# A two-layer hybrid block on one core: fewer, packed loads at the start, and the first two projections interleaved

## The chip, the core and the metric

The kernel runs on one core of a Trainium2 chip. TensorE (PE) multiplies, VectorE (DVE), ScalarE (ACT) and GpSimd (POOL) work element by element, and SyncE (SP) issues nearly all loads. The metric is the device time of one execution in microseconds.

## The reference

Two layers. Each normalises the stream (256 context and 256 latent tokens of 1024 channels), scales and shifts it by a modulation vector, projects it by one wide matrix, runs three token mixers on the parts (a state-space scan, "SSD", differential attention, and an mLSTM), and merges them by gates:

```
shift, scale, gate = split(silu(c) @ w_mod + b_mod, 3)       # c_ctx for the context tokens
h = rms_norm(x, norm_g) * (1 + scale) + shift
p = split_cols(h @ w_in, IN_SIZES)     # x, B, C, z, dt, q, k, v, ..., ig, fg, gates
ya = ssd_branch(p[0], p[1], p[2], ...)      # conv + silu of x, B, C; dt; a scan in both directions
yb = diff_branch(...);  yc = mlstm_branch(...)
mixed = sum_i sigmoid(gates_i) * (y_i @ w_branch[i])
x = x + gate * (mixed @ w_out)
```

## The kernel before

Every product in float32 is made of three products of float32r halves: a weight tile `raw` is rounded to `whi` by ACT (L117), DVE subtracts to get `wlo` (L83, the helper `tt`), and the stream h likewise has `hh` and `hl`. A **granule** is half a weight block: 4 of the 8 slices of 128 input channels by 256 columns, 512 KB, loaded into one of three `raw` buffers. `proj_ch` (L164) makes two blocks of 128 output channels by 512 tokens from two granules, 24 matmuls of 512 columns for each granule (lines L177 to L179).

The start of layer 0 is `mod_pair` (L243): twice eight loads of `w_mod` (512 KB, `wm`), each followed at once by its two matmuls (`mod_mm`, L226), which lay slice k into column tile k mod 4 of one PSUM bank. ACT copies the bank (`modrow`, L262), and `mod_tail` (L235) folds the four column tiles into modulation columns `modc`. The first pair gives shift and scale for slices 0 to 3 of h, the second for slices 4 to 7. The last three loads of the second pair go into `raw` buffers. Between the `wm` loads `few_loads` issues the small parameters: rows of `prow` (bias, conv weights and gains, later turned into columns by `columns`, L395), and the tables of `narrow` (L287: `gcol`, `gctx`, `dbc`, `lamt`) and `rope`.

`turn` (L488) transposes normalised tokens (L493), applies modulation on ACT (`hf`), rounds on POOL (`hh`) and subtracts on DVE (`hl`). Then come the gate matmuls (L553 to L555) on the narrow weights `wsm`, six loads of 4 or 16 columns (L544); a long chain on their 64 rows (L586 to L649) gives the SSD's decays, and its first use of PE is the transpose at L627. The blocks follow in the order `bc_proj(0)`, `x_proj(0, 0)`, `x_proj(0, 1)`, `ssd_core(0)`, the q, k, v blocks, and the same for the second group.

The order on every engine is made by a scheduler before the run, from priorities: the bands put loads and evacuations first (0), mixer work second (1) and the matmuls of projections last (2), so that these fill what the others leave free. On the chip each engine keeps that order. Every load in turn takes one of eight completion counters, and SP issues it only when the load eight places earlier has landed. PSUM has three banks `acc`, three `pe` and two `pm`.

Of the kernel before, what the change touches and what calls it, by code (L numbers as in the profile page):

```python
# [18 lines left out]
D = 1024  # L19
P = 128  # L20
# [9 lines left out]
NR = 64  # L30
ACC, PE_, PM = 3, 3, 2
# [3 lines left out]
def hybrid_backbone_kernel(ctx: ExitStack, tc: tile.TileContext, A, out, dbg=None):  # L35
# [128 lines left out]
    def proj_ch(srcs, lhs, ranges, evac, halves=False, gr=None):  # L164
# [3 lines left out]
        with band(2):  # L168
            for i in range(2):
                ps.append(pacc())  # L170
# [11 lines left out]
        if not halves:  # L182
            for k0, hi, lo in gr:
                with band(2):
                    for i in range(2):
                        go(i, k0, hi, lo, *ranges[i], True, True)
        else:
# [8 lines left out]
        for i in range(2):  # L196
            with band(0):
                evac(i, ps[i])

# [31 lines left out]
    def mod_tail(l, cbs, row):  # L231
        with band(2):
# [3 lines left out]
            for x, cb in enumerate(cbs):  # L236
                r = 16 * l + 12 + cb // 3
# [5 lines left out]
    def mod_pair(l, cbs, pool, bufs, rbufs, between=None, each=None, end=False):  # L243
        with band(2):
            ps = pacc()
            for x, cb in enumerate(cbs):
                if x and between:
                    between()
                for k0 in range(0, KT, 2):
                    if end and x and k0 >= 2:  # L250
                        wm = mk(wts, [P, 2, 512], "raw", bufs=3)
                    else:
                        wm = mk(pool, [P, 2, 512], "wm", bufs=bufs)
# [6 lines left out]
                    mod_mm(ps, x, k0, wm)  # L260
# [26 lines left out]
    def narrow(l, pool):  # L287
# [3 lines left out]
        lamt = mk(pool, [P, 4, 64], "lamt", bufs=1)  # L291
        lp = mk(pool, [P, 2, 64], "lp", bufs=1)
# [47 lines left out]
    prow = [mk(setup, [16, 1536], f"prow{l}") for l in range(depth)]  # L340
    with band(0):
# [5 lines left out]
        for l in range(depth):  # L347
            V.memset(prow[l], 0.0)
# [3 lines left out]
        few = []  # L352
        for l in range(depth):
            w_ = prow[l]

            few += [
                (w_[12:14, :], A["b_mod"][l].rearrange("(a n) -> a n", a=2)),
                (w_[8:9, 0:D], A["norm_g"][l : l + 1]),
                (w_[0:3, :], A["ssd_conv_w"][l]),
                (w_[3:4, :], A["ssd_conv_b"][l : l + 1]),  # L360
                (w_[4:7, 0:D], A["ml_conv_w"][l]),
                (w_[7:8, 0:D], A["ml_conv_b"][l : l + 1]),
                (w_[9:10, 0:D], A["ssd_norm_g"][l : l + 1]),
                (w_[10:11, 0:D], A["ml_norm_g"][l : l + 1]),
                (w_[11:12, 0:P], A["diff_subln_g"][l : l + 1]),
            ]
# [9 lines left out]

# [15 lines left out]
    def columns(l):  # L392
        pc = pm()
        for k in range(12):
            T.transpose(pc[:, 16 * k : 16 * k + 16], prow[l][:, k * P : (k + 1) * P], ident[0:16, 0:16])  # L395
        pl_ = pcols[:, :, 16 * l : 16 * l + 16]
        V.tensor_copy(pl_, pc[:, 0:192].rearrange("p (k a) -> p k a", a=16))

        tsc(pl_[:, :, 0:8], pl_[:, :, 0:8], 0.5, ALU.mult)
        lam_init = 0.8 - 0.6 * math.exp(-0.3 * l)  # L400
        tsc(pl_[:, 0, 11:12], pl_[:, 0, 11:12], 0.5 * (1.0 - lam_init), ALU.mult)
# [1013 lines left out]
```

## Time and profile before

| | us |
|---|---|
| median of three runs (lowest, highest) | 1688.14 (1687.44, 1690.84) |
| the profiled execution, and its span | 1688.44, 1686.7 |
| PE busy | 1649.9 |
| mean granted TensorE clock | 0.992 |

The times are to be read with the profile's own terms: a span runs from the first to the last instruction, a busy engine works on something, and an instruction's row names what ended the idle time ahead of it. Matmul records overlap, so a full PE still has its pace in the distance between starts: 0.227 us for a matmul of 512 columns at the full clock.

### The profile page before, as it was taken

Reading aid. Unit: us, or ns where it says so; the run is one execution under the profiler, and the core shown is the slowest. Engines: PE = TensorE matmul, PEld = TensorE weight load, DVE = VectorE, ACT = ScalarE, POOL = GpSimd, SP = SyncE. Lnnn points to the kernel's source line nnn. Section 1 sums busy time; section 2 is a strip of 40 time slices with the busy share of each in tenths; the row PEclk is TensorE's granted clock in tenths of the full one; section 3 lists DMA queues with packets and bytes.
Section 4 is the critical chain, followed back from the end, with each engine's and each line's share of the span. In section 5 each row is a group of like instructions: output and inputs, shape, how many; then the busy total and the mean of one; then the engine's idle time right before and its main releaser. Section 6 shows DMA issues by size and latency. Waiting matters only on the chain. (4 is left out here: it accounts for less than half of the span.)

```text
span 1686.7 us, 28784 instructions
## 1 busy us (share of the span) xinstructions
PE 1649.9 (98%) x11288; PEld 1470.5 (87%) x11288; DVE 1093.0 (65%) x2175; ACT 765.4 (45%) x1497; POOL 185.1 (11%) x232
## 2 busy tenths in 40 slices
PE   6999999999999999999999999999999999999998
PEld 2798789999899999977777789988899999999998
DVE  4787887767864776523334355796887767775565
ACT  3467534554554543422223233556455555444453
POOL 0114331001100000000010001022122011000100
PEclk8999999999999999999999999999999999999999
DMA  8445322222223222453544442344342325336654
GB/s 273 119 134 160 88 79 79 69 71 63 78 63 101 79 85 64 128 187 93 182 136 128 161 135 59 93 127 135 107 116 76 100 76 141 110 101 176 183 168 150
DMA packets 203653, 197.00 MB, mean 117 GB/s; under 512 B 21855, under 2 KB 184033, under 8 KB 203517
## 3 DMA queue, kind: packets, MB, share of 16 engines
q1 hardware_dynamic: 203516, 195.16, 39.4%
q8 instruction: 89, 1.46, 0.3%
q14 instruction: 48, 0.39, 0.1%
HBM read 193.29 MB, written 1.84 MB: 116 GB/s over the span
## 5 line engine op out<-in xcount | busy, mean ns | idle before, releaser
L83 DVE TENSOR_TENSOR wlo<-raw,whi 128x1024 fp32r<-128x1024 f32 x274 | 347.1, 1267 | 313.8 <-ACT whi L117 312.4
L147 PE MATMUL acc<-wlo,hh 128*128 128x256 f32 x1728 | 504.4, 292 | 0.0
L146 PE MATMUL acc<-whi,hh 128*128 128x256 f32 x1728 | 502.3, 291 | 0.0
L148 PE MATMUL acc<-whi,hl 128*128 128x256 f32 x1728 | 501.5, 290 | 0.0
L117 ACT CAST whi<-raw 128x1024 fp32r<-128x1024 f32 x274 | 287.1, 1048 | 378.1 <-PE acc L178 253.0
L147 PEld LDWEIGHTS acc<-wlo,hh 128*128 128x128 f32 x1728 | 330.1, 191 | 12.5 <-issue 9.5
L148 PEld LDWEIGHTS acc<-whi,hl 128*128 128x128 f32 x1728 | 330.2, 191 | 12.2 <-issue 10.6
L146 PEld LDWEIGHTS acc<-whi,hh 128*128 128x128 f32 x1728 | 329.8, 191 | 11.0 <-issue 8.5
L177 PE MATMUL acc<-hh,whi 128*128 128x512 f32 (+1 forms) x712 | 254.1, 359 | 1.3 <-DVE cv_a L80 1.3
L178 PE MATMUL acc<-hl,whi 128*128 128x512 f32 (+1 forms) x712 | 253.7, 357 | 0.2 <-DVE hl L83 0.2
L179 PE MATMUL acc<-hh,wlo 128*128 128x512 f32 (+1 forms) x712 | 253.1, 357 | 0.0
L177 PEld LDWEIGHTS acc<-hh,whi 128*128 128x128 f32 x712 | 135.0, 191 | 28.3 <-issue 5.9
L178 PEld LDWEIGHTS acc<-hl,whi 128*128 128x128 f32 x712 | 135.4, 190 | 19.4 <-issue 2.4
L179 PEld LDWEIGHTS acc<-hh,wlo 128*128 128x128 f32 x712 | 135.3, 190 | 19.3 <-issue 1.8
L177 PE MATMUL acc<-yh,whi 128*128 128x512 f32 (+1 forms) x384 | 128.7, 338 | 0.0
L178 PE MATMUL acc<-yl,whi 128*128 128x512 f32 (+1 forms) x384 | 128.2, 336 | 0.0
L179 PE MATMUL acc<-yh,wlo 128*128 128x512 f32 (+1 forms) x384 | 128.1, 336 | 0.0
L179 PEld LDWEIGHTS acc<-yh,wlo 128*128 128x128 f32 x384 | 71.9, 188 | 8.3
L178 PEld LDWEIGHTS acc<-yl,whi 128*128 128x128 f32 x384 | 72.1, 188 | 8.0
L968 ACT ACTIVATE E<-pe,nmax 128x512 f32<-128x512 f32 (+1 forms) x96 | 58.7, 616 | 44.8 <-DVE nmax L966 44.6
L177 PEld LDWEIGHTS acc<-yh,whi 128*128 128x128 f32 x384 | 72.0, 188 | 7.3
L811 ACT ACTIVATE ex<-ex,col 128x128 f32<-128x128 f32 x192 | 60.4, 393 | 34.8 <-POOL ex L766 31.0
(302 smaller groups left out, 2429.3 us busy)
## 6 DMA issues: line engine op xcount, KB each, us to landing
raw<-in_w_in_dram SPq DMA_DIRECT2D x192, 512.0 KB
raw<-in_w_branch_dram SPq DMA_DIRECT2D x48, 512.0 KB
wm<-in_w_mod_dram SPq DMA_DIRECT2D x45, 512.0 KB
raw<-in_w_in_dram SPq DMA_DIRECT2D x48, 256.0 KB
ex<-acs_d SPq DMA_DIRECT2D x32, 256.0 KB
raw<-in_w_out_dram SPq DMA_DIRECT2D x16, 512.0 KB
ex<-acs_d SPq DMA_DIRECT2D x32, 128.0 KB
pw<-nm_d SPq DMA_DIRECT2D x8, 256.0 KB
```

What stands on the lines that cost most here:

```text
L83: (eng or V).tensor_tensor(out=o, in0=a, in1=b, op=op)
L117: S.copy(hi, raw)
L146: T.matmul(o, lhsT=xh[:, k, sl], rhs=hi[:, j, :], start=(k == 0 and i == 0), stop=False)
L147: T.matmul(o, lhsT=xh[:, k, sl], rhs=lo[:, j, :], start=False, stop=False)
L148: T.matmul(o, lhsT=xl[:, k, sl], rhs=hi[:, j, :], start=False, stop=(k == KT - 1 and i == 1))
L177: T.matmul(o, lhsT=hi[:, j, cs], rhs=xh[:, k, a:b], start=(k == 0 and first), stop=False)
L178: T.matmul(o, lhsT=hi[:, j, cs], rhs=xl[:, k, a:b], start=False, stop=False)
L179: T.matmul(o, lhsT=lo[:, j, cs], rhs=xh[:, k, a:b], start=False, stop=(k == KT - 1 and final))
L811: S.activation(ex[:, c, :], ex[:, c, :], AF.Exp, bias=col[:, LDT, c, d, h : h + 1])
L968: S.activation(e_, o, AF.Exp, bias=ng[:, m : m + 1], accum_out=rs[:, m : m + 1])
```

## The change

The parameter rows of both layers are loaded together, ten loads in the place of eighteen, into `mrow_` (modulation bias and norm gain) and `prow` (the rest), with column numbers `C_CW` to `C_NORM` in the place of `16 * l + r`. The tables of `narrow(0)` and `rope` move from between the modulation loads to behind them. The gate weights come in two loads (32 and 16 columns) into `wnr`, and three DVE copies put them into `wsm`, in both layers. All modulation loads have buffers of their own (11 `wm`), and `mod_pair` holds one load back, so that two loads' matmuls, four column tiles, stand together. The first granule of `x_proj(0, 0)` is loaded ahead of the second modulation pair, like that of `bc_proj(0)`; the two blocks of layer 0 alternate by granules, the second one in `pe` banks. `turn` in layer 0 goes slice by slice over both halves of the tokens and uses `pm` banks alone.

```diff
+    mrow_ = mk(setup, [6, 1536], "mrow_")
+    prow = mk(setup, [22, 1536], "prow")
-    prow = [mk(setup, [16, 1536], f"prow{l}") for l in range(depth)]
...
-            few += [
-                (w_[12:14, :], A["b_mod"][l].rearrange("(a n) -> a n", a=2)),
-                (w_[8:9, 0:D], A["norm_g"][l : l + 1]),
-                (w_[0:3, :], A["ssd_conv_w"][l]),
...
-            if l == 0:
-                few += [(selm, A["k_selm"]), (sgn, A["k_sgn"])]
-                nar = narrow(0, setup)
-                few += nar[0]
-                few += [(rope, A["k_rope"].rearrange("a t p d -> p a t d"))]
+        few = [
+            (mrow_[0:4, :], A["b_mod"].rearrange("l (a n) -> (l a) n", a=2)),
+            (mrow_[4:6, 0:D], A["norm_g"]),
+            (selm, A["k_selm"]),
+            (prow[0:6, :], A["ssd_conv_w"].rearrange("l k n -> (l k) n")),
+            (prow[6:8, :], A["ssd_conv_b"]),
+            (prow[8:14, 0:D], A["ml_conv_w"].rearrange("l k n -> (l k) n")),
+            (prow[14:16, 0:D], A["ml_conv_b"]),
+            (prow[16:18, 0:D], A["ssd_norm_g"]),
+            (prow[18:20, 0:D], A["ml_norm_g"]),
+            (prow[20:22, 0:P], A["diff_subln_g"]),
+            (sgn, A["k_sgn"]),
+        ]
...
     def mod_pair(...):
+                held = []
                 for k0 in range(0, KT, 2):
-                    if end and x and k0 >= 2:
-                        wm = mk(wts, [P, 2, 512], "raw", bufs=3)
-                    else:
-                        wm = mk(pool, [P, 2, 512], "wm", bufs=bufs)
+                    wm = mk(pool, [P, 2, 512], "wm", bufs=bufs)
...
-                    mod_mm(ps, x, k0, wm)
+                    held.append((k0, wm))
+                    if len(held) == 2:
+
+                        for k_, w_ in held:
+                            mod_mm(ps, x, k_, w_)
+                        held = []
...
-    mods = [mod_pair(0, (0, 2), setup, 8, 2, load_x, lambda: few_loads(2))]
-
-    first_gr = granules(bc_cols(0, 0))
-    first_gr = chain([next(first_gr)], first_gr)
+    mods = [mod_pair(0, (0, 2), setup, 11, 2, load_x, lambda: few_loads(1))]
+
+    first_gr = [granules(bc_cols(0, 0)), granules([A["w_in"][0][:, O_X : O_X + 256]])]
+    first_gr = [chain([next(g)], g) for g in first_gr]
     mods += [
-        mod_pair(0, (1, 3), setup, 8, 2, None, lambda: few_loads(3), end=True),
+        mod_pair(0, (1, 3), setup, 11, 2, None, lambda: few_loads(1)),
     ]
     with band(0):
+        columns(mrow_, 22)
         few_loads(99)
-        columns(0)
+        columns(prow, 0)
...
             def turn(kh, s):
-                for k in range(4 * kh, 4 * kh + 4):
-                    pt = (pe if k % 2 else pm)()[:, 0:256]
+                for k in kh:
+                    pt = (pe if k % 2 and l else pm)()[:, 0:256]
...
-                    for s in range(2):
-                        turn(kh, s)
+                    for k in range(4 * kh, 4 * kh + 4):
+                        for s in range(2):
+                            turn((k,), s)
...
+            wnr = mk(wts, [P, KT, 48], "raw", bufs=3)
             wsm = mk(wts, [P, KT, P], "raw", bufs=3)
             V.memset(wsm, 0.0)
-            pieces = ((0, O_DT, 16), (16, O_FG, 4), (32, O_DT + 16, 16), (48, O_FG + 4, 4), (80, O_IG, 4), (112, O_IG + 4, 4))
-            for c, o, n in pieces:
-                nc.sync.dma_start(wsm[:, :, c : c + n], w_in[:, o : o + n].rearrange("(k p) n -> p k n", p=P))
+            for c, o, n in ((0, O_DT, 32), (32, O_IG, 16)):
+                nc.sync.dma_start(wnr[:, :, c : c + n], w_in[:, o : o + n].rearrange("(k p) n -> p k n", p=P))
+
+            v4 = lambda a: a.rearrange("p k (d r) -> p k d r", d=2)
+            for c, o, n in ((0, 0, 16), (16, 40, 4), (80, 32, 4)):
+                h_ = 64 * (c // 64)
+                V.tensor_copy(v4(wsm[:, :, h_ : h_ + 64])[:, :, :, c % 64 : c % 64 + n], v4(wnr[:, :, o : o + 2 * n]))
+            if l == 0:
+
+                scr = mk(wts, [P, 1024], "raw", bufs=3)
...
+                for p_ in nar[0][4:] + nar[0][:4]:
+                    nc.sync.dma_start(*p_)
+                nc.sync.dma_start(rope, A["k_rope"].rearrange("a t p d -> p a t d"))
...
+            first = l + g + b == 0
+            return proj_ch([wcol(O_X + 512 * g + 256 * b)], hT, [(0, 512)] * 2, f, gr=first_gr[1] if first else None, bank=pe if first else None)
...
-        bc_proj(0)
-        x_proj(0, 0)
-        x_proj(0, 1)
+        if l == 0:
+            run(zip_longest(bc_proj(0), x_proj(0, 0)))
+        else:
+            run(bc_proj(0))
+            run(x_proj(0, 0))
+        run(x_proj(0, 1))
```

What the scheduler makes of it shows in the order of three engines. SP in the second modulation pair, first before: `wm` and the last `raw` are modulation loads, all others small.

```order
L255 DMA wm<-in_w_mod_dram 128x2x512
L375 DMA prow_99<-in_norm_g_dram 1x1024
L375 DMA prow_99<-in_ssd_conv_w_dram 3x1536
L375 DMA prow_99<-in_ssd_conv_b_dram 1x1536
L255 DMA wm<-in_w_mod_dram 128x2x512
L375 DMA prow_99<-in_ml_conv_w_dram 3x1024
L375 DMA prow_99<-in_ml_conv_b_dram 1x1024
L375 DMA prow_99<-in_ssd_norm_g_dram 1x1024
L255 DMA raw<-in_w_mod_dram 128x2x512
L375 DMA prow_99<-in_ml_norm_g_dram 1x1024
L375 DMA prow_99<-in_diff_subln_g_dram 1x128
L255 DMA raw<-in_w_mod_dram 128x2x512 x2
```

The same place now; `raw` are the two first granules.

```order
L260 DMA wm<-in_w_mod_dram 128x2x512
L378 DMA prow<-in_ml_conv_w_dram 6x1024
L260 DMA wm<-in_w_mod_dram 128x2x512
L378 DMA prow<-in_ml_conv_b_dram 2x1024
L260 DMA wm<-in_w_mod_dram 128x2x512
L378 DMA prow<-in_ssd_norm_g_dram 2x1024
L130 DMA raw<-in_w_in_dram 128x4x128 x2
L130 DMA raw<-in_w_in_dram 128x4x256
L260 DMA wm<-in_w_mod_dram 128x2x512
L378 DMA prow<-in_ml_norm_g_dram 2x1024
L260 DMA wm<-in_w_mod_dram 128x2x512
L378 DMA prow<-in_diff_subln_g_dram 2x128
```

Two or three small loads stood between two modulation loads, and now one; the granule for x has come in.

PE in the first blocks, before: L177 to L179 are the B/C block, L553 to L555 the gates, L395 the row columns of layer 1.

```order
L553 MATMUL pe<-hh,whi 128x512
L554 MATMUL pe<-hl,whi 128x512
L555 MATMUL pe<-hh,wlo 128x512
L179 MATMUL acc<-hh,wlo 128x512
L177 MATMUL acc<-hh,whi 128x512
L178 MATMUL acc<-hl,whi 128x512
L395 MATMUL pm<-ident,prow_99 128x16 x12
L553 MATMUL pe<-hh,whi 128x512
L554 MATMUL pe<-hl,whi 128x512
L555 MATMUL pe<-hh,wlo 128x512
L553 MATMUL pe<-hh,whi 128x512
```

Now: L492 are transposes of x, L565 to L567 the gates, L179 to L181 the B/C block in `acc` and the x block in `pe`.

```order
L492 MATMUL pm<-ident,xin 128x128 x4
L565 MATMUL pe<-hh,whi 128x512
L179 MATMUL acc<-hh,whi 128x512 x2
L566 MATMUL pe<-hl,whi 128x512
L567 MATMUL pe<-hh,wlo 128x512
L180 MATMUL acc<-hl,whi 128x512
L181 MATMUL acc<-hh,wlo 128x512
L180 MATMUL acc<-hl,whi 128x512
L181 MATMUL acc<-hh,wlo 128x512
L179 MATMUL pe<-hh,whi 128x512
L180 MATMUL pe<-hl,whi 128x512
L179 MATMUL pe<-hh,whi 128x512
```

The gate matmuls, once in two runs of four slices, now go slice by slice between those of two blocks, and transposes of x have moved in.

DVE about the second set of modulation columns (`modc`, `ga`), before; `raw` here is the zeroed tile of gate weights.

```order
L83 TENSOR_TENSOR hl<-hf,hh 128x256 x8
L541 MEMSET raw 128x1024
L83 TENSOR_TENSOR modc<-acc,pcols 128x8 x2
L87 TENSOR_SCALAR ga<-modc 128x8
L83 TENSOR_TENSOR ga<-ga,pcols 128x8
L83 TENSOR_TENSOR wlo<-raw,whi 128x1024
L83 TENSOR_TENSOR hl<-hf,hh 128x256 x4
```

Now the copies from `wnr` (L545), and the lambda product in a `raw` buffer:

```order
L85 TENSOR_TENSOR gcs<-rope,gctx 128x64
L85 TENSOR_TENSOR gsn<-rope,gctx 128x64
L545 COPY raw<-raw 128x8x2x16
L545 COPY raw<-raw 128x8x2x4 x2
L85 TENSOR_TENSOR hl<-hf,hh 128x256
L530 MEMSET sv 64x12
L85 TENSOR_TENSOR modc<-acc,pcols 128x8 x2
L85 TENSOR_TENSOR raw<-raw 128x128
L85 TENSOR_TENSOR hl<-hf,hh 128x256
L89 TENSOR_SCALAR ga<-modc 128x8
L328 TENSOR_REDUCE ls<-raw 128x2
L85 TENSOR_TENSOR wlo<-raw,whi 128x1024
```

Between the splits of h (`hl`) the modulation columns now come after the copies of the gate weights.

## Rows read from the trace of the kernel before

**Rows 1.** The page's engines: busy us, share of the span, instructions.

```profile
PE 1649.9 (98%) x11288; PEld 1470.5 (87%) x11288; DVE 1093.0 (65%) x2175; ACT 765.4 (45%) x1497; POOL 185.1 (11%) x232
```

**Rows 2.** Stretches: us, engines' busy time (instructions), PEclk, DMA share, GB/s.

```profile
14.00:20.00 6.00, 0.06 (x1) 0.06 (x2) 2.12 (x14) 5.25 (x16) 0.00 (x0) 0.63 1.00 372
20.00:28.00 8.00, 8.00 (x30) 3.00 (x30) 6.12 (x29) 0.30 (x2) 0.00 (x0) 0.50 0.85 274
20.00:43.40 23.40, 21.00 (x90) 7.31 (x90) 14.62 (x53) 5.92 (x12) 3.92 (x8) 0.80 0.81 261
46.14:50.00 3.86, 3.86 (x12) 3.05 (x12) 0.58 (x4) 0.57 (x1) 0.00 (x0) 0.56 0.93 114
110.00:190.00 80.00, 74.05 (x413) 59.74 (x412) 61.14 (x84) 55.48 (x150) 36.65 (x38) 1.00 0.52 151
165.00:190.00 25.00, 21.24 (x95) 14.99 (x94) 19.65 (x24) 16.35 (x42) 14.78 (x13) 1.00 0.37 103
1005.00:1045.00 40.00, 40.00 (x339) 40.00 (x339) 22.11 (x31) 11.64 (x21) 2.81 (x6) 1.00 0.38 86
```

**Rows 3.** Timeline: start, duration, engine, line, operation, tiles [idle before <-releaser].

```profile
40.88 1.05 PE L226 MATMUL acc<-raw,cst 128*32 128x512 f32 x4 [1.06 <-DMA raw<-in_w_mod_dram]
...
42.20 1.05 PE L226 MATMUL acc<-raw,cst 128*32 128x512 f32 x4 [0.27 <-DMA raw<-in_w_mod_dram]
...
43.48 1.05 PE L226 MATMUL acc<-raw,cst 128*32 128x512 f32 x4 [0.23 <-DMA raw<-in_w_mod_dram]
44.58 0.59 ACT L262 COPY modrow<-acc 128x512 f32<-128x512 f32 x1 [6.91 <-PE acc L226]
...
45.22 1.05 PE L235 MATMUL acc<-selm,modrow 128*128 128x4 f32 x8 [0.69 <-ACT modrow L262]
...
46.14 0.61 PE L177 MATMUL acc<-hh,whi 128*128 128x512 f32 x1
```

**Rows 4.** Timeline of SP's load queue, 14 to 18 us.

```profile
14.70 0.57 SPq L375 DMA_DIRECT2D sgn<-in_k_sgn_dram  x1
...
17.30 0.38 SPq L255 DMA_DIRECT2D wm<-in_w_mod_dram  x1
```

**Rows 5.** Timeline of PE: modulation matmuls, two records to each.

```profile
19.94 1.92 PE L226 MATMUL acc<-wm,cst 128*32 128x512 f32 x2 [6.90 <-DMA wm<-in_w_mod_dram]
...
26.50 1.94 PE L226 MATMUL acc<-wm,cst 128*32 128x512 f32 x8
```

**Rows 6.** Timeline of PE inside the first blocks.

```profile
53.06 0.38 PE L493 MATMUL pm<-ident,xin 128*128 128x128 f32 x2
...
53.63 0.47 PE L553 MATMUL pe<-hh,whi 128*128 128x512 f32 x1
...
56.92 0.39 PE L178 MATMUL acc<-hl,whi 128*128 128x512 f32 x1
57.24 0.91 PE L395 MATMUL pm<-ident,prow 16*128 16x16 f32 x12
58.08 0.50 PE L553 MATMUL pe<-hh,whi 128*128 128x512 f32 x1
...
60.49 0.39 PE L554 MATMUL pe<-hl,whi 128*128 128x512 f32 x1
60.72 0.39 PE L555 MATMUL pe<-hh,wlo 128*128 128x512 f32 x1
...
72.04 0.47 PE L177 MATMUL acc<-hh,whi 128*128 128x512 f32 x1 [0.51 <-DVE cv_a L80]
```

**Rows 7.** Timeline: the narrow loads and the cast that waits for them.

```profile
43.16 3.76 SPq L544 DMA_DIRECT2D raw<-in_w_in_dram  x6
...
49.43 1.05 ACT L117 CAST whi<-raw 128x1024 fp32r<-128x1024 f32 x1 [4.26 <-DMA raw<-in_w_in_dram]
```

**Rows 8.** Timeline: the gate row chain's first step and its first transpose.

```profile
61.87 0.77 ACT L92 ACTIVATE r_u<-pe,gcol,sgn 64x512 f32<-64x512 f32 x1
...
92.53 0.27 PE L627 MATMUL pm<-ident,r 128*128 128x128 f32 x1
```

More of the change, by code (lines that the diff above doesn't have):

```diff
@@ L2 @@
 from contextlib import ExitStack, contextmanager
-from itertools import chain
+from itertools import chain, zip_longest
 import concourse.bass as bass
@@ L162, in proj_tok, with proj_ch @@
                 evac(p, ps[p].rearrange("p (t n) -> p t n", t=2))
-    def proj_ch(srcs, lhs, ranges, evac, halves=False, gr=None):
+    def proj_ch(srcs, lhs, ranges, evac, halves=False, gr=None, bank=None):
         xh, xl = lhs
@@ L198, in proj_ch, with run @@
                 evac(i, ps[i])
+    def run(steps):
+        for _ in steps:
+            pass
     def rsqrt(src, n, scale, eps, pp=P, pool_=True):
@@ L241, in mod_tail, with mod_pair @@
                 )
-    def mod_pair(l, cbs, pool, bufs, rbufs, between=None, each=None, end=False):
+    def mod_pair(l, cbs, pool, bufs, rbufs, between=None, each=None):
         with band(2):
@@ L284, in mod_steps, with narrow @@
         yield
-    def narrow(l, pool):
+    def narrow(l, lamt, lp):
         lam_init = 0.8 - 0.6 * math.exp(-0.3 * l)
@@ L510, in hybrid_backbone_kernel @@
                     norm(s)
-                    for kh in range(2):
-                        turn(kh, s)
+                    turn(range(KT), s)
         hT = (hh, hl)
@@ L517, in hybrid_backbone_kernel @@
         if l == 0:
-            with band(0):
-                for l_ in range(1, depth):
-                    columns(l_)
             setup.release()
@@ L733, in f @@
                 if i == 0:
-                    uB[g] = conv_silu(ps, 512, 8 + g, 0, sp, "uB", 1)
+                    uB[g] = conv_silu(ps, 512, 8 + g, C_CW, C_CB, sp, "uB", 1)
                 else:
-                    uC[g] = conv_silu(ps, rng_c[1] - rng_c[0], 10 + g, 0, sp, "uC", 1)
-            proj_ch(
+                    uC[g] = conv_silu(ps, rng_c[1] - rng_c[0], 10 + g, C_CW, C_CB, sp, "uC", 1)
+            return proj_ch(
                 bc_cols(l, g), hT, [(0, 512), rng_c], f,
-                halves=(g == 0 and l > 0), gr=first_gr if g == 0 and l == 0 else None,
+                halves=(g == 0 and l > 0), gr=first_gr[0] if g == 0 and l == 0 else None,
             )
@@ L882, in hybrid_backbone_kernel @@
         XT[1] = mk(sp, [P, NT, 512], "XT", bufs=2)
-        bc_proj(1)
-        x_proj(1, 0)
-        x_proj(1, 1)
+        run(bc_proj(1))
+        run(x_proj(1, 0))
+        run(x_proj(1, 1))
         ssd_core(1)
@@ L1209, in hybrid_backbone_kernel @@
             with band(0):
-                nar = narrow(l + 1, lpool)
+                nar = narrow(l + 1, mk(lpool, [P, 4, 64], "lamt"), mk(lpool, [P, 2, 64], "lp"))
                 for p_ in nar[0]:
@@ L1239, in transposed @@
             return yh, yl
-        for b, (y, sc_) in enumerate(((ya, lambda k: pcol(k, 9)), (yb, lambda k: pcol(0, 11)), (yc, lambda k: pcol(k, 10)))):
+        for b, (y, sc_) in enumerate(((ya, lambda k: pcol(k, C_SSDN + l)), (yb, lambda k: pcol(0, C_SUB + l)), (yc, lambda k: pcol(k, C_MLN + l)))):
             with band(1):
@@ L1249, in fg @@
                     S.activation(tg[i], ps[:, 0:nqt], AF.Tanh, scale=0.5)
[L1251 removed]
+                run(proj_ch([wcol(O_G + b * D + cb * 256)], hT, [(lo_, 512)] * 2, fg))
                 def fb(i, ps, tg=tg, b=b, cb=cb):
```

70 lines of the change are left out of this document (30 added, 40 removed).

## The prediction

> **What bounds the kernel now.** The first view is the page's list of engines: PE is busy 98% of the span, every other engine far less [rows 1]. The time is therefore the moment at which dense matmuls begin, plus their work, plus the holes between them. The change touches the beginning, so the stretches of the start come next. From 14 to 20 us the loads run at 372 GB/s, from 20 to 43.4 us at 261 GB/s [rows 2]. In the second stretch small loads stand between the large ones. Third, the timeline of the last modulation loads: PE takes each pair of matmuls when its 512 KB load has landed, at 40.88, 42.20 and 43.48 us; ACT copies the sums at 44.58, PE folds them at 45.22, and the first matmul of the first projection starts at 46.14 us [rows 3]. From there PE is nearly full, at a granted clock of 0.56 up to 50 us and 1.00 afterwards [rows 2]. So the bound of the start is the load queue, and whatever brings the 43.48 forward brings the end forward, unless PE finds a new hole later.
>
> **The change part by part.** *Fewer loads.* SP gives every load one of eight completion counters in turn, so a load is issued only when the one eight places earlier has landed. That shows from 14.70 to 17.30 us, when the first three loads of x and ctx free a place each: 2.60 / 2 = 1.30 us per 512 KB where large loads follow each other [rows 4]. The last two modulation loads, issued back to back, come 1.32 and 1.28 us apart as well [rows 3]. Over the whole stretch the pace is worse. From the first of those landings (14.70) to the last modulation load in use (43.48) there are 16 loads of 512 KB (three of x and ctx, twelve of modulation, one granule of w_in in two halves): 28.78 / 16 = 1.80 us each. Between them the program has 25 small loads, 1.56 per large one; the excess of 0.50 us is thus 0.32 us per small load. After the change there are 17 large loads in that stretch (a granule of w_in for x comes in) and 9 small ones, 0.53 each: 1.30 + 0.53 x 0.32 = 1.47 us. Ahead of the first landing four fewer row loads are queued, 4 x 0.32 = 1.3 us, so it comes at 13.4. The last modulation load is then in use at 13.4 + 17 x 1.47 = 38.4 us: **-5.1 us**. The bounds: at 1.30 per load 35.5 us (-8.0), at the old 1.80 and the old start 45.3 us (+1.8, one load more for nothing). I take the middle because the number of small loads, which I hold for the cause, falls to a third and not to zero.
>
> *Two granules in all four column tiles.* At the granted clock of 0.50 of 20 to 28 us [rows 2], a record of two matmuls in one column tile took 1.92 us and one of eight in all four 1.94 us [rows 5]. Held back in pairs of loads, the matmuls of the first half of the phase cost PE half as much, but PE only waits for loads there, so nothing comes of it. Behind the last load the order still has that load's two matmuls (1.05 us), the copy and the fold: 46.14 - 43.48 = 2.66 us, unchanged. If the sparser work leaves PE at the low clock there, the pair costs 0.87 us more and the fold up to 1.05 us: between 0 and +1.9. I take **+0.4**, near the row at full clock, since transposes and row columns now also lie in that stretch.
>
> *The first two blocks by halves.* Both first granules (B/C and x) are on hand, so more matmuls need only the first four slices of h. The block itself has as many matmuls as before. The low clock at its beginning costs 3.86 x 0.44 = 1.7 us before [rows 2] and stays; without it -1.7. The second set of row columns (57.24 to 58.08, and 0.93 us from the end of the matmul ahead) goes into the load phase [rows 6]: **-0.9**. Against that, transposes of x are now fourteen more behind the first matmul (20 instead of 6), because they use two PSUM banks only, the others being taken by the second block. Six took 53.06 to 53.63, 0.095 us each [rows 6]: **+1.3**. The wait for a free accumulator before 72.04 (0.51 us) [rows 6] may go, since the second block has banks of its own, or return one block later: 0, and -0.5 in the range.
>
> *The narrow weights and the small parameters.* Six narrow loads ran from 43.16, and the ACT cast waited for them until 49.43 us [rows 7]. Now two loads carry the same bytes, and DVE copies them into place. They, rope and lambda stand behind the last modulation load on SP, and on DVE those copies stand ahead of the second set of modulation columns. Counting from the last landing: issue some 2.4 us later, landed 2.5 us after that (as 46.92 to 49.43), three copies of 0.3 us, two splits of h and the columns, about 7.5 us in all. PE asks for the split of the third slice after 2.66 us, twelve matmuls at 0.45 us (twice the 0.23 of full clock, 60.49 to 60.72 [rows 6]) and four transposes, about 8.9 us. The cover is 1.4 us, so I take 0; each us later costs a us, up to +3. In layer 1 the same loads fall into a stretch, 1005 to 1045 us, in which PE is full [rows 2]: 0.
>
> *What is late next.* The gate matmuls (dt, i, f) now alternate with the two blocks. Counting each matmul of the order at its spacing in this trace (0.227 us per 512 columns, as from 60.49 to 60.72 [rows 6]), they ended 13.3 us of PE work after the first matmul, and now 27.7. Their row chain on ACT and DVE took from 61.87 to the first transpose at 92.53 us, 31 us [rows 8]. The scheduler has moved that transpose too, from 44.0 to 63.4 us of PE work: 35.8 us of matmuls now cover the chain instead of 30.7. I take 0 for the scan stage behind it, whose holes are 80.0 - 74.05 = 6.0 us now [rows 2]; between -4 and +10.
>
> The sum against the profiled execution (1688.44 us, a span of 1686.7 and 1.7 around it): -5.1 + 0.4 - 0.9 + 1.3 = -4.3, so 1684.1 us. The median of the three runs lies 0.3 lower (1688.14), so I say **1683.8 us**.
>
> **The rivals.** *The queue gains nothing.* The row loads cost by what they carry to one or two partitions, not by their number. Packed, they bring the same bytes, and those of both layers now come ahead of the block in any case. For it speaks that the busy share of the DMA engines stays at 0.81 while the rate falls to 261 GB/s [rows 2], so the small loads occupy the engines and do not only leave them idle. Against it: lambda, the q/k gains, rope and most gate parameters leave the stretch altogether. Then the last load is used at about 43.5, and 0 + 0.4 - 0.9 + 1.3 gives 1688.9 us, no change. The Trainium skill (DMA: Bandwidth & Descriptors, the section on why a DMA increments its semaphore by 16) points this way: a load runs on at most as many engines as divide its slowest dimension, the lowest-numbered ones, so all the two-row loads would share the same two. The trace before has no row per DMA engine that would show it.
>
> *Slower: the scan stage starves.* The place is the SSD stage, where PE runs in order and DVE feeds it. In the worst stretch before (165 to 190 us) PE is idle 3.76 of 25 us, 15% [rows 2]. The new order has 4 us less of projection matmuls between the steps of the first group (59.7 against 63.7 us of PE work). If that made DVE the bound over both groups, some 122 us of PE work, 15% would be 18 us against 8 now: +10, so 1694 us. It decides from 4 us on, where it eats the gain. Against it: DVE is busy 61 of the 80 us of that stage, and 19.7 of the 25 in its worst stretch [rows 2].
>
> *More than I count.* The queue runs at 1.30 us per load (35.5 us, -8.0) and PE, now busier ahead of the block, keeps the clock (-1.7): -8.0 - 1.7 - 0.9 + 1.3 = -9.3, so 1678.8 us. For it: the mean clock from 20 to 43.4 us was 0.80, with 0.50 in the first eight of them, so it was near full from 28 us on with PE far from dense [rows 2]; against it: nine small loads remain.
>
> **How the numbers follow.** My forecast 0.52, its own range 1681.5 to 1686.5; the idle queue 0.20; the starved scan 0.11; the fast one 0.17. A measurement here tells a change from none at about 0.2%, 3.4 us: faster is below 1684.8. Two thirds of my forecast lie there (0.34), with the fast rival and a little of the queue's 0.53; no change gets 0.36, slower 0.11. The range from 1678.5 to 1690.5 leaves out the starved scan and the ends of the fast one.
>
> **What would show it.** The first matmul of the block at 41 to 42 us instead of 46.14, the last modulation matmul at 38 to 39 with large loads landing about 1.5 us apart, the clock at half for the first 3 to 4 us of the block, no row columns inside it, and holes of about 6 us in the scan stage, some 80 us long and starting later than 110 us. If the block starts at 45 or 46, the loads were not the cause that I make them; if it starts at 41 and the end does not move, the holes between the first scan step and the end of the second group must have grown, which a table by stages would show.

## The result and the profile after

The changed kernel takes 1703.11 us (median of four runs, 1702.67 to 1705.38) against 1688.72: a ratio on record of 1.0093, 95% interval 1.0077 to 1.0109. (The 1688.72 has a fourth run beside the three ahead of the prediction, and the ratios on record, here and below, are not the quotients of the two medians.) That is 14 us slower by the medians and 16 by the ratio, where 1683.8 was forecast and 1690.5 was the end of the range.

The page of the profile after has PE as full as before, and its busy time only 2.7 us longer [rows 1]:

```profile
PE 1652.6 (97%) x11288; PEld 1473.9 (87%) x11288; DVE 1088.9 (64%) x2180; ACT 766.4 (45%) x1497; POOL 185.6 (11%) x232
```

The span grew by 14.3 us (1686.7 to 1701.0), so 11.6 us of it are new idle time of PE, and a table by stretches of the kernel after finds where. The columns are those of [rows 2].

```profile
14.00:20.00 6.00, 2.10 (x6) 0.37 (x8) 4.06 (x21) 3.83 (x12) 0.00 (x0) 1.00 1.04 384
28.00:36.00 8.00, 8.00 (x36) 3.98 (x33) 1.85 (x10) 0.56 (x1) 0.41 (x1) 0.50 0.93 336
36.00:41.35 5.35, 5.35 (x21) 1.08 (x16) 1.17 (x5) 1.13 (x2) 0.82 (x2) 0.80 0.25 50
44.00:48.00 4.00, 4.00 (x21) 3.33 (x21) 3.63 (x16) 1.90 (x4) 0.97 (x3) 1.00 0.58 143
110.00:190.00 80.00, 76.98 (x448) 65.15 (x447) 60.90 (x116) 54.19 (x142) 24.56 (x30) 0.98 0.52 154
530.00:620.00 90.00, 76.79 (x516) 69.62 (x515) 56.38 (x165) 39.25 (x97) 6.73 (x9) 0.94 0.26 74
```

The last row is the loss: 13.2 us of idle PE between 530 and 620 us, some 500 us behind what the diff touches at the start, and a lower clock around it. The same stretch of the kernel before is full:

```profile
530.00:620.00 90.00, 90.00 (x618) 84.25 (x617) 60.51 (x175) 43.36 (x100) 6.34 (x10) 1.00 0.31 90
```

At that place layer 0 goes from attention to the mLSTM: I call it the switch. The timeline of the kernel before shows how it passes there: the attention's last sum (`ssB`, on DVE), the mLSTM's first product (`uq`, `uk`, L1098), then projections, and 7.7 us after that product the first use of the mLSTM's weights `pw` (L1112).

```profile
539.69 0.69 DVE L988 TENSOR_REDUCE ssB<-rt 128x4 f32<-128x512 f32 x1 [3.84 <-ACT rt L987]
...
542.02 1.05 PE L1098 MATMUL pm<-uq,uk 128*128 128x128 f32 x8
542.83 0.36 PE L146 MATMUL acc<-whi,hh 128*128 128x256 f32 x1
...
549.71 0.60 PE L1112 MATMUL pm<-va,pw 128*128 128x257 f32 x2
```

After, no projection lies between the two (the lines are now L1114 and L1128). Rows of the timeline of all engines:

```profile
563.63 0.61 ACT L1003 ACTIVATE rt<-pm 128x512 f32<-128x512 f32 x1
564.28 0.69 DVE L1004 TENSOR_REDUCE ssB<-rt 128x4 f32<-128x512 f32 x1 [7.21 <-ACT rt L1003]
564.30 1.16 PE L1114 MATMUL pm<-uq,uk 128*128 128x128 f32 x8 [1.24 <-ACT rt L1003]
...
565.05 1.77 SPq L777 DMA_DIRECT2D pw<-nm_d  x4
...
568.32 3.40 DVE L82 SCALAR_TENSOR_TENSOR yb<-yb,riB,zz 128x128 f32<-128x128 f32 x8
...
569.72 3.38 ACT L1122 ACTIVATE pw<-pw,mlc 128x128 f32<-128x128 f32 x11 [3.63 <-POOL pw L779]
...
571.64 1.13 DVE L85 TENSOR_TENSOR pw<-pw,scT 128x512 f32<-128x512 f32 x1
...
572.83 0.80 PE L1128 MATMUL pm<-va,pw 128*128 128x257 f32 x1 [7.37 <-DVE pw L85]
```

The chain from the attention's last sum through the load of `pw`, ACT and DVE has not become longer: 8.6 us from `ssB` to the first use of `pw`, against 10.0 before. Before, 44 projection matmuls of the order stood behind the first product; after, none, and PE waits 1.24 us for the product and 7.37 for `pw`. These are 8.6 of the 13.2 us. Another 3.9 us lie ahead of them, in three waits of PE among the attention's last steps, two of them for a projection's accumulator that DVE has yet to read:

```profile
545.34 0.50 PE L179 MATMUL acc<-hh,whi 128*128 128x512 f32 x1 [1.66 <-DVE cv_a L82]
...
553.12 1.16 PE L998 MATMUL pm<-p,aT 128*128 128x128 f32 x8 [0.73 <-ACT aT L996]
...
555.73 0.39 PE L148 MATMUL acc<-whi,hh 128*128 128x256 f32 x1 [1.46 <-DVE cv_a L82]
```

The projections had run earlier: up to the mLSTM's first product PE ran 2784 projection matmuls (L148 to L150 and L179 to L181), and 2658 before (L146 to L148 and L177 to L179). The reading that the experiments put to the test is that PE had used them to fill while the mixers (SSD, attention), which came late, were not ready. The lateness can be followed in three single rows of the kernel after, the gate chain's first step and first transpose (61.87 and 92.53 before [rows 8]) and the first attention step, whose row of before stands last:

```profile
72.90 0.77 ACT L94 ACTIVATE r_u<-pe,gcol,sgn 64x512 f32<-64x512 f32 x1
...
110.76 0.27 PE L639 MATMUL pm<-ident,r 128*128 128x128 f32 x1
...
302.47 0.39 PE L980 MATMUL pe<-kh,qh 64*128 64x256 f32 x2
```

```profile
277.79 0.38 PE L964 MATMUL pe<-kh,qh 64*128 64x256 f32 x1
```

They are 11, 18 and 25 us late, although the first block starts 2.1 us earlier (44.03).

### The profile page after: what moved, and what is told of

Read it like the earlier page. It is cut to its first block, busy times and chain, and to the rows that moved or that the text cites. A ratio compares the mean times of both kernels' runs of the same rounds, so it can differ in the third digit from the quotient of the medians.

```text
span 1701.0 us, 28771 instructions
## 1 busy us (share of the span) xinstructions
PE 1652.6 (97%) x11288; PEld 1473.9 (87%) x11288; DVE 1088.9 (64%) x2180; ACT 766.4 (45%) x1497; POOL 185.6 (11%) x232
## 5 line engine op out<-in xcount | busy, mean ns | idle before, releaser
L148 PE MATMUL acc<-whi,hh 128*128 128x256 f32 x1728 | 502.6, 291 | 2.8 <-DVE cv_a L82 1.5
L150 PE MATMUL acc<-whi,hl 128*128 128x256 f32 x1728 | 504.7, 292 | 0.0
L148 PEld LDWEIGHTS acc<-whi,hh 128*128 128x128 f32 x1728 | 331.3, 192 | 13.9 <-issue 8.1
L150 PEld LDWEIGHTS acc<-whi,hl 128*128 128x128 f32 x1728 | 331.3, 192 | 12.1 <-issue 10.2
L179 PE MATMUL acc<-hh,whi 128*128 128x512 f32 (+1 forms) x696 | 245.7, 357 | 2.8 <-DVE cv_a L82 1.7
L180 PE MATMUL acc<-hl,whi 128*128 128x512 f32 (+1 forms) x696 | 247.7, 357 | 0.2 <-DVE hl L85 0.2
L181 PE MATMUL acc<-hh,wlo 128*128 128x512 f32 (+1 forms) x696 | 247.3, 357 | 0.0
L179 PEld LDWEIGHTS acc<-hh,whi 128*128 128x128 f32 x696 | 131.3, 190 | 28.9 <-issue 5.6
L181 PEld LDWEIGHTS acc<-hh,wlo 128*128 128x128 f32 x696 | 131.7, 189 | 19.4 <-issue 2.5
L180 PEld LDWEIGHTS acc<-hl,whi 128*128 128x128 f32 x696 | 131.8, 189 | 18.2 <-issue 1.9
L179 PE MATMUL acc<-yh,whi 128*128 128x512 f32 (+1 forms) x384 | 128.8, 338 | 0.0
L181 PE MATMUL acc<-yh,wlo 128*128 128x512 f32 (+1 forms) x384 | 128.1, 336 | 0.0
L181 PEld LDWEIGHTS acc<-yh,wlo 128*128 128x128 f32 x384 | 71.9, 188 | 8.3
L179 PEld LDWEIGHTS acc<-yh,whi 128*128 128x128 f32 x384 | 72.0, 188 | 7.3
```

Of the source, the lines that this page charges most:

```text
L148: T.matmul(o, lhsT=xh[:, k, sl], rhs=hi[:, j, :], start=(k == 0 and i == 0), stop=False)
L150: T.matmul(o, lhsT=xl[:, k, sl], rhs=hi[:, j, :], start=False, stop=(k == KT - 1 and i == 1))
L179: T.matmul(o, lhsT=hi[:, j, cs], rhs=xh[:, k, a:b], start=(k == 0 and first), stop=False)
L180: T.matmul(o, lhsT=hi[:, j, cs], rhs=xl[:, k, a:b], start=False, stop=False)
L181: T.matmul(o, lhsT=lo[:, j, cs], rhs=xh[:, k, a:b], start=False, stop=(k == KT - 1 and final))
```

## The experiments

The first theory: late gates make late mixers, these use up the projections, and the switch lies open. The rivals: the loads do it, or an accident of the order. "Left" is the number of projection matmuls that the order has between the mLSTM's first product and its first use; "switch" is the time from the first block's first matmul to that product, and "hole" PE's idle time from 530 to 620 us, both in the profiled run.

| kernel | left | switch | hole | median us | ratio to before (95%) |
|---|---|---|---|---|---|
| before | 44 | 495.9 | 0 | 1688.72 | |
| changed | 0 | 520.3 | 13.2 | 1703.11 | 1.0093 (1.0077, 1.0109) |
| e1 blocks in turn | 24 | 510.0 | 6.5 | 1696.62 | 1.0050 (1.0035, 1.0064) |
| e2 late gates alone | 21 | 509.4 | 6.5 | 1697.41 | 1.0055 (1.0038, 1.0072) |
| e3 old slice order | 24 | 517.0 | 5.0 | 1694.73 | 1.0037 (1.0022, 1.0052) |
| e4 pm banks alone | 21 | 508.0 | 6.5 | 1695.40 | 1.0046 (1.0029, 1.0062) |
| e7 packed rows alone | 24 | 511.7 | 6.5 | 1695.07 | 1.0037 (1.0023, 1.0052) |
| e9 row chain first | 24 | 512.4 | 6.5 | 1697.27 | 1.0058 (1.0046, 1.0071) |
| e5 = e1, more stock | 44 | 511.4 | 2.4 | 1686.46 | 0.9995 (0.9984, 1.0005) |
| e11 = e7, more stock | 44 | 513.8 | 2.1 | 1691.55 | 1.0017 (1.0007, 1.0027) |
| e10 changed, more stock | 0 | 523.5 | 11.0 | 1702.07 | 1.0086 (1.0072, 1.0100) |
| e12 before, more stock | 44 | 493.0 | 0 | 1683.77 | 0.9981 (0.9971, 0.9992) |

**e1.** The changed kernel, its blocks one after the other.

```diff
-        if l == 0:
-            run(zip_longest(bc_proj(0), x_proj(0, 0)))
-        else:
-            run(bc_proj(0))
-            run(x_proj(0, 0))
+        run(bc_proj(0))
+        run(x_proj(0, 0))
-        pt = (pe if k % 2 and l else pm)()[:, 0:256]
+        pt = (pe if k % 2 else pm)()[:, 0:256]
```

> Edit: the changed kernel with its first two blocks one after the other again, in acc banks, and the transposes in pe and pm banks; the packed loads, the held pairs and the two narrow loads stay. Theory (late mixers): the alternating blocks delay the gate matmuls, by that every mixer step up to the switch from attention to the mLSTM, where PE has run out of projections. In the order the gates now end 14.5 us of PE work behind the block's first matmul (11.5 before the change, 26.3 after), and 24 projection matmuls stand between the mLSTM's first product and its first use (44 before, none after). So the first block starts near 44 us as after the change, the gate chain starts some 8 us earlier than after it, and the hole at the switch shrinks from 13 us to 4 to 9: 1691 to 1696 us. Rival A (the hole comes from the loads, that is from SP's new queue): it stays, 1701 to 1703 us. Rival B (the hole is an accident of the order that has nothing to do with the blocks): also 1701 or more, or no hole at all.

Half of the hole went, with all loads in place, so the loads are not the cause of that half; e7 below is about the other. The time is 0.6 us above the range, and the first block came at 46.67 us, not near 44 (45.48 in e5, which has the same start).

**e2.** The kernel before, with only the priority of the gate matmuls lowered, behind the first two blocks.

```diff
-        with band(2):
+        bands[3] = bands[2] + (200 if l == 0 else 0)
+        with band(3 if l == 0 else 2):
             pg = pe()
```

> Edit: the kernel before with one thing changed, the gate matmuls get a priority behind the first two blocks. Loads, blocks, transposes as before. In the order the gates end 27.9 us of PE work behind the block's first matmul, as late as after the change (26.3), and 21 projection matmuls are left at the switch from attention to the mLSTM (44 before). Theory (late mixers): the first block still starts at 46 us, the gate chain some 15 us later than before, the scan stage's holes do not grow, and a hole of 4 to 9 us opens at the switch, 500 us further on: 1692 to 1698 us. Rival A (the loads make the hole): no hole, 1688 to 1690 us. Rival C (late gates are covered, as the prediction held): 1688 to 1690 us.

Late gates alone open a hole 500 us further on. PE's stretch, and the wait that makes most of the 6.5 us of idle time (who waits for whom: us in total, times, longest):

```profile
530.00:620.00 90.00, 83.50 (x561) 76.77 (x561) 58.00 (x163) 40.88 (x94) 6.36 (x9) 0.96 0.29 80
```

```profile
PE acc L146 <- DVE zz L80: 5.4, 1, 5.4
```

The projection that could fill waits for an accumulator. Its holder waits for a place for its gated product `zz`, of which there are two, both kept until the attention's last result (`riB`) multiplies them. So the projections that may run ahead of the attention's end are a stock of a fixed size. The same single wait of 5.4 to 5.5 us makes the hole of e1, e4, e7 and e9.

**e3 and e4.** In the changed kernel the old order of the slices; in the kernel before, transposes on two banks.

```diff
-                    for k in range(4 * kh, 4 * kh + 4):
-                        for s in range(2):
-                            turn((k,), s)
+                    for s in range(2):
+                        turn(range(4 * kh, 4 * kh + 4), s)
```

> Edit: the changed kernel, but the slices of h are made in the old order, four slices of one half of the tokens and then of the other, in place of both halves slice by slice; the blocks still alternate. In the order the gates end 22.0 us of PE work behind the first matmul (26.3 after the change), the first attention step stands 196.6 us behind it (202.8), and 24 projection matmuls are left at the switch (none). Theory (late mixers): the hole shrinks from 13 to 5 to 10 us, 1694 to 1699 us. Rival A (loads): 13 us stay, 1701 to 1704 us.

```diff
-                    pt = (pe if k % 2 else pm)()[:, 0:256]
+                    pt = (pe if k % 2 and l else pm)()[:, 0:256]
```

> Edit: the kernel before with one thing changed, the first layer's transposes of x use the two pm banks alone, as after the change. In the order the gates end 16.9 us of PE work behind the first matmul (11.5 before), the first attention step 188.1 (175.8), and 21 projection matmuls are left at the switch (44). Theory (late mixers): a hole of 3 to 9 us at the switch, 1691 to 1698 us. Rivals A and C: transposes move by some 1.3 us and nothing else, 1688 to 1691 us.

Both as the theory had it: one edit in the first 60 us decides over some 8 us of the time, near 550 us.

**e7.** The kernel before with the packed rows alone (the diff's `few`, `columns` and column numbers).

> Edit: the kernel before with the packed row loads alone (the rows of both layers in ten loads and one set of row columns fewer in the block); six narrow loads, the tables between the modulation loads, no held pairs, first blocks in turn, eight wm buffers and the last loads in raw buffers, as before. Theory: fewer row loads let the load queue run faster, so the last modulation load lands before 40 us, but PE may be at half clock then: the first block at 42 to 46 us. In the order the gates end 14.2 us behind the first matmul (11.5 before) and 24 projections are left at the switch: a hole of 4 to 7 us there. Together 1688 to 1694 us. If the packing were harmless to the order, 1684 to 1686 us.

The first block starts at 44.12 us, 2 us earlier, and the hole costs three times that; the time is 1.1 us above the range. So the packed loads are enough for a hole too, by the order that the scheduler makes with them: 24 projections are left and 6.5 us idle, the same as what e1, which keeps them, had left.

**e9.** In the kernel before, the gates' row chain gets the priority of loads.

```diff
-        with band(1):
+        with band(0):
             row = lambda n, b=1: mk(rp, [NR, 512], n, bufs=b)
```

> Edit: the kernel before with one thing changed, the gates' row chain has the priority of loads and evacuations instead of that of mixers. Loads, blocks and gate matmuls stay where they were: in the order the gates still end 11.5 us of PE work behind the first matmul and the chain's transpose stands at 42.4 us, but the first attention step comes out at 185.2 us (175.8 before), and 24 projections are left at the switch (44). Theory in its narrow form (late gates make the hole): gates are early, so no hole, 1687 to 1690 us. Theory in its wide form (whatever brings the mixers late against the projections empties the stock): a hole of 5 to 7 us at the switch, 1692 to 1696 us.

The gates' first transpose is at 90.36 us, earlier than before, the first attention step at 287.50, and the hole is there (the time is 1.3 us above the range of the wide form):

```profile
530.00:620.00 90.00, 83.47 (x562) 76.82 (x561) 57.66 (x164) 40.44 (x95) 6.54 (x9) 0.96 0.27 80
```

So my theory falls in its narrow form: late gates are enough for the hole, but not needed. What counts is how far the projections have run when the attention ends.

**e5, e10 to e12.** The stock itself made larger.

```diff
-            zz = mk(ev, [P, 2, 256], "zz", bufs=2)
+            zz = mk(ev, [P, 2, 256], "zz", bufs=3)
-                    sq = mk(ev, [P, 2, 256], "sq", bufs=2)
+                    sq = mk(ev, [P, 2, 256], "sq", bufs=1)
```

> Edit: the kernel of e1 (blocks in turn), with three buffers in place of two for the gated products zz of the projections, and one in place of two for the squares sq, to make room. Nothing of the start is touched: gates and attention stand where they stood in e1. In the order 44 projection matmuls are left at the switch from attention to the mLSTM (24 in e1, 44 in the kernel before). Theory (late mixers eat the stock of projections): the attention starts as late as in e1 (some 242 us behind the first block), yet the hole at the switch falls from 6.5 to 0 to 2 us: 1688 to 1692 us. Rival (the switch is late by a chain on VectorE or a load, and PE's order has no part in it): the hole stays at 6 to 7 us, 1696 to 1697 us. The single sq buffer may cost up to 1 us elsewhere.

Some 9 us faster than e1 by the two ratios (10 by the medians) and 1.5 us below the range, with its gate chain and its switch about where they stood in e1 (511.4 us against 510.0). The row of the stretch, 6.5 us of idle PE in e1:

```profile
530.00:620.00 90.00, 87.63 (x573) 78.30 (x571) 60.27 (x173) 43.34 (x101) 6.67 (x9) 1.00 0.31 86
```

> Edit: the changed kernel with three zz buffers and one for sq, as in e5. The gates and the attention stay as late as they are; in the order no projection is left at the switch, but the switch itself stands behind 435.2 us of PE work in place of 429.8, since more projections could run ahead of it. Theory (the stock of projections that may run ahead of the switch is limited by these buffers): 5.4 us more of them cover 5 us of the 13 us hole: 6 to 9 us are left, 1695 to 1699 us against 1703. Rival (the hole is a latency that more projections can't cover, since none is left in the order at the switch): 13 us and 1702 to 1704 us.

A miss: two of the 13 us went, not four to seven, and the time lies in the rival's range. The 5.4 us of projections ran ahead and the waits ahead of the mLSTM's first product are gone, but PE still waits 6.68 us for `pw` (7.37), and new waits of 3 us stand behind it. Here a larger stock, all of which ran ahead, did not cover the switch.

> Edit: the kernel before with three zz buffers and one for sq and nothing else. In the order the attention starts at 176.0 us (175.8 before) and 44 projections are left at the switch, as before. Theory (the buffers matter only where the stock runs out): no hole before, none now, 1686 to 1690 us, no change. Rival (the buffers make the kernel faster by themselves, by which e5 would be explained without the switch): 1679 to 1684 us.

No hole, as expected, but 0.19% faster (0.08 to 0.29), the fastest of all, and within the rival's range, though only just. In the profiled run PE is busy 2.7 us less (its clock is 1.00 in the first 3.8 us of the block, 0.56 before [rows 2]) and idle 2 us less. That the extra buffer does this isn't shown. Of e5's 9 us, then, some 3 may come from the buffers without the switch; its hole is 4.1 us smaller than e1's.

> Edit: the kernel before with the packed row loads (as e7) and three zz buffers and one for sq (as e5). In the order the gates end at 14.2 us, the attention starts at 187.1, 44 projections are left at the switch. Theory: the first block at 44 us as in e7, the hole 0 to 2.5 us in place of 6.5, so e7's 1695 less 6 to 10: 1685 to 1689 us; it beats the kernel before (1687 to 1689) if the two us of the start arrive at the end. Rival (the single sq buffer takes it back): 1690 or more.

The hole shrank as expected, but the time is above the range and in that of the rival (the single `sq` buffer takes it back), which is thus not ruled out. In this run the first block started at 44.80 us, and at 45.26 in e12, which has the loads of before; the attention started at 287.14.

**The start.** Five runs on the first block, which came at 44.03 us and not at 41 to 42.

```diff
-                    if len(held) == 2:
+                    if len(held) == 1:
```

> Edit: the changed kernel without holding a modulation load back: each load's two matmuls run as soon as it has landed, two column tiles at a time. The order of all later work is that of the changed kernel. Theory (PE at half clock bounds the start): the eight loads that PE takes at half clock cost it twice as much, so the first block starts 1 to 5 us later than 44 us, unless the clock stays up because PE is busier ahead; the hole at the switch stays 13 us: 1703 to 1708 us. As the prediction had it (pairs save nothing, since PE waits for loads): no difference, 1703 us.

1703.84 us (1.0093, 1.0077 to 1.0108), first block 44.57: no difference, though not because PE waits for loads. From 27 to 43 us PE has the same sequence of rows in both kernels, none more than 0.6 us apart: its order puts transposes between the two loads of most pairs, and takes the last two loads together (1.07 us) whether they are held or not.

```diff
+                            for _ in range(more):
+                                T.matmul(hot[0:32, :], lhsT=cst[:, k_, 0:32], rhs=w_[:, 0, :], start=True, stop=True)
```

> Edit: the changed kernel with matmuls into a spare bank that nothing reads: one behind each pair of modulation loads and three where PE waits for the loads of x and for the first granules (13 to 18 us and 24 to 27.5 us after the change). Theory (the start is now bound by PE at half clock): the clock stays full from 20 us on, the last modulation load is used at 35 to 37 us in place of 41.35, the first block starts at 37.5 to 40 us in place of 44.03; the hole at the switch stays (no matmul is left there in the order), so 1697 to 1700 us against 1703. Rival (the loads are the bound as before): the first block at 44 us, 1703 us.

Inconclusive: the clock fell to 0.50 from 32 to 36 us all the same, the first block came at 44.16; 1700.39 us (1.0070, 1.0050 to 1.0091), between the ranges of theory and rival.

```diff
                         for k_, w_ in held:
-                            mod_mm(ps, x, k_, w_)
+                            if between or l or (x == 0 and k_ < 4) or (x == 1 and k_ >= 4):
+                                mod_mm(ps, x, k_, w_)
```

> Edit: the changed kernel without the matmuls of four of the eight loads of the second modulation pair (the loads themselves stay; the shift and scale of four slices are computed from half of their inputs). The work left out is at most 4 us of PE's 1652. What it tells apart is the start after the change. Theory (PE at half clock, not the load queue, sets the first block after the change): the last modulation load is in use at 35 to 38.5 us (41.35), the first block starts at 38 to 41 us (44.03), the end comes 3 to 5 us earlier, 1698 to 1700 us, the hole at the switch stays 13 us. Rival (the last load lands at 41 us): the first block at 43.5 to 44 us, 1702 to 1703 us.

A miss for both: 1704.05 us (1.0087, 1.0072 to 1.0102), the first block at 45.03. The profile shows why leaving out half of the second pair's matmuls gave nothing:

```profile
37.25 1.14 PE L493 MATMUL pm<-ident,xin 128*128 128x128 f32 x4 [0.23 <-ACT hf L94]
...
38.60 1.15 PE L493 MATMUL pm<-ident,xin 128*128 128x128 f32 x4 [0.20 <-ACT hf L94]
...
42.38 1.05 PE L233 MATMUL acc<-wm,cst 128*32 128x512 f32 x4
```

The transposes of the first slices stand ahead of the last loads' matmuls in PE's order, and on two banks each waits for ACT to empty one, 1.35 us for each four transposes (one slice of h), with PE at 0.52 of its clock from 28 to 41 us.

```diff
-                                T.matmul(hot[0:32, :], lhsT=cst[:, k_, 0:32], ...)
+                                T.matmul(hot, lhsT=ident, rhs=w_[:, 0, :], start=True, stop=True)
```

> Edit: the changed kernel with unread matmuls in PE's first waits, as in e6, but over all 128 columns of the array, five in place of three in each of the two long waits. Theory (what PE did ahead sets the clock, and matmuls of 32 columns did too little for it in e6): the granted clock stays above 0.8 from 28 to 38 us (0.50 after the change, 0.5 to 0.7 in e6), the first block starts at 38 to 42 us, 1697 to 1701 us. Rival (the clock falls there whatever PE does): 0.5 again, the first block at 44 to 46 us, 1702 to 1706 us.

The clock was 1.00 from 14 to 44 us, as the theory had it, but the first block came at 44.16 us and the time was 1704.19 us (1.0090, 1.0069 to 1.0111). Unread matmuls stand in the very stretch that was to become shorter, and may have taken what the clock gave; e15 leaves those out.

> Edit: as e14, but the unread matmuls stand only in PE's two long first waits (five each, 13 to 18 us and 23.5 to 28 us); in the second pair there are none, so that PE has there just the work of the changed kernel. In e14 the clock stayed full, but 3.3 us of unread matmuls lay in the stretch that they were to shorten. Theory (after the change PE bounds the start, by its work at the granted clock and by the transposes that wait on two banks, and not the load queue): at full clock the last modulation load is in use at 37.5 to 40 us and the first block starts at 40 to 42.5 us (44.03 after the change, 44.16 in e14); the hole at the switch stays 13 us, 1699 to 1702 us. Rival (a load or the transposes alone set it): 43.5 us or later at a full clock. If the clock falls again, neither is told.

1700.34 us (1.0064, 1.0045 to 1.0083), the first block at 42.62 and the hole 12.8 us. PE over 28 to 38 us in the changed kernel, and then in e15:

```profile
28.00:38.00 10.00, 10.00 (x38) 4.16 (x34) 2.26 (x10) 0.56 (x1) 0.41 (x1) 0.50 0.76 272
```

```profile
28.00:38.00 10.00, 10.00 (x59) 4.11 (x58) 3.79 (x14) 3.62 (x7) 2.98 (x6) 1.00 0.74 268
```

At full clock PE is still busy without a hole from 28 us to its last modulation matmul at 39.96. So after the change PE's own work, in its order, sets the start; of the gain that was missing, the half clock holds 1.4 us (one run against one; e10, which starts like the changed kernel, had its first block at 43.62).

## Why the prediction was wrong, step by step

*What is late next: this step failed.* It said "35.8 us of matmuls now cover the chain instead of 30.7. I take 0 for the scan stage behind it". For that stage the words held: PE's idle time from 110 to 190 us fell from 6.0 to 3.0 us, where I had expected 6 and had priced growth as the slower rival. The stage now starts some 18 us later, so the wider comparison counts more: 8.8 us before and 7.6 after from 110 to 290 us, and none in either from 290 to 530. But the matmuls that cover a late mixer are taken from a stock of projections. I saw the transpose move from 44.0 to 63.4 us of PE work and asked only whether PE would stay busy over it, not what PE would have left later. The 13.2 us around the switch are the price (e1 to e4: fewer left in the order, and a hole; e5: as late a switch with the stock refilled, and 2.4 us).

*Fewer loads: mis-sized, and the bound moved.* The queue was faster than I took it for: the rate is 384 GB/s from 14 to 20 us and 336 from 28 to 36, then 50, so the loads are in by some 36 us, near the early bound of 35.5 that I had worked out. But the last modulation load was used at 41.35 us and not 38.4. "So the bound of the start is the load queue" is the step that failed here: PE waits for loads up to 28 us (3.66 of 8.00 us busy from 20 us on), but from 28 us it is full, up to 38 us at 0.50. Its low clock at 20 to 28 us with 8.00 of 8.00 us busy [rows 2] had shown in the kernel before that PE can be full there, and I read that stretch as one of loads. The term is -2.1 us in the place of -5.1, and even that is between single runs: e9 and e12, which load like the kernel before, used their last modulation load at 42.68 and 42.61 us, not at 43.48. Nor is the number of row loads shown to be what held the queue. In e7, with the packed rows but the tables still between the large loads, the queue was no faster than before (274 GB/s from 20 to 28 us [rows 2], 252 from 28 to 36). The first two rows are e7's, the third that of the kernel before:

```profile
20.00:28.00 8.00, 6.81 (x38) 2.53 (x38) 4.64 (x15) 1.53 (x2) 0.00 (x0) 0.80 0.86 258
28.00:36.00 8.00, 7.33 (x25) 1.95 (x26) 2.88 (x16) 2.03 (x6) 0.88 (x3) 0.63 0.80 235
```

```profile
28.00:36.00 8.00, 7.85 (x42) 3.04 (x40) 4.60 (x17) 3.95 (x8) 1.98 (x4) 0.92 0.84 252
```

The faster queue of the changed kernel came with the tables moved behind the loads and a buffer for every load as well; which of these made it faster, no run tells.

*The smaller terms.* Behind the last load 2.68 us pass up to the first block (44.03 - 41.35), against 2.66: 0, not +0.4. The clock at the block's start is 1.00, so the 1.7 us of low clock that I had left in the sum are gone. The second set of row columns went into the load phase, where PE is now full, so nothing shows that its -0.9 was gained. The transposes behind the first matmul cost what I counted, 0.09 us each (four from 46.87 to 47.23 us), but they too were moved out of a stretch in which PE is full, so nothing shows that their +1.3 was a loss. The cover for the narrow weights held: the cast ran at 44.73, the first gate matmul at 48.69, without a wait.

*The rivals.* "The queue gains nothing" is refuted by the rates for the whole change, but not for the packing alone, as e7's rows show. "The scan stage starves" had the sign and neither place nor price: 1694 for the scan, 1703 by the switch. "More than I count" was right on the queue, and the end did not follow.

The sum as measured, 14.3 us: 13.2 more idle around the switch, 1.6 less idle in all other stretches, 2.7 more busy, with a lower clock around the hole (0.94 over 530 to 620 us).

What stays open: why the scheduler's order jumps between such states, and so by which step each edit at the start uses up the projections. e9 had the SSD's first state product 2 us earlier (109.36 us against 111.34) and moved the attention by 9.7 us; e15 began its attention 12.6 us earlier than the changed kernel and still had none left at the switch. The kernel before has the best order of those tried but e12, with e5 level.

## What to carry to other kernels

Where dense work fills the gaps of a serial chain, ask not only whether a gap is covered but how much filler is left for the last one: work that a late chain consumes early is missing where that chain next lies open. When a scheduler makes the order from priorities, compare the whole order, stage by stage, and count the filler at each handover, however far it is from the edit. And before a start is called bound by loads, look whether PE is full there at a low clock.

## What the runs showed of the hardware

Unread matmuls of 32 output columns in PE's waits (e6) did not keep the clock: 0.66 over 28 to 38 us, with PE busy 10.0 of these 10. With unread matmuls over all 128 columns, in e15 five in each of the two waits and none behind, it was 1.00 over the same stretch. The number of them differs too (three and five), so which of the two did it isn't told apart. A busy PE alone is thus no sign of a full clock: in the changed kernel it was full from 28 to 38 us at 0.50.
